# Forty-nine TensorE steps, 115 VectorE steps and 61 ScalarE steps of a hand-ordered decoder layer change places

## The chip, the cores and the metric

The kernel runs on one core of a Trainium2 chip. The metric is the device time of one execution in microseconds (us). Three runs of the kernel before gave 623.32, 624.0 and 621.71 us, a median of 623.32. One more execution was profiled; every row below comes from it.

The engines are named as the profile names them: PE is TensorE (PEld its weight loads), DVE is VectorE, ACT is ScalarE, POOL is GpSimd, SP is SyncE, on whose queue nearly all transfers are issued. "L1591" is line 1591 of the kernel before.

## The reference: what is computed

One layer of a decoder on a sequence of 512 tokens with 1024 features, float32 throughout:

```python
h = rms_norm(x, attn_pre_norm[l])
mix = hybrid_mixer(h, ...)      # differential attention + native sparse attention
x = x + rms_norm(mix, attn_post_norm[l])
h = rms_norm(x, ffn_pre_norm[l])
f = (jax.nn.silu(h @ w_gate[l]) * (h @ w_up[l])) @ w_down[l]
x = x + rms_norm(f, ffn_post_norm[l])
```

`w_gate` and `w_up` are 1024 x 2816, `w_down` is 2816 x 1024. The mixer projects the tokens once, runs four differential-attention heads and eight heads of native sparse attention, and projects back.

## The kernel before, in words

Every float32 operand of a product is split into a high part, rounded to fp32r, and a low part, the remainder, and three fp32r matmuls (high*high, high*low, low*high) stand for one float32 product. So a weight tile goes through a fixed path: a transfer into one of three `raw` slots (512 KB, `load_...`), a copy on ACT that makes the high part (`high_...`), a subtraction on DVE that makes the low part (`low_...`), then the matmuls. A `raw` slot is free for the next transfer when its last reader, often the `low_...` step, is done.

The layer has two parts. The first is the mixer: projections (`F...`, `K...`, `v...`), differential heads (`D...`) and sparse heads (`N...`). The second is the two norms and the feed-forward network (FFN). In the FFN a Strassen-like scheme saves products: of the gate and the up weights of one of 22 column strips f it forms sums (`sum_ff.f.n`, DVE, L1548 to L1555), splits four operands (`high_ff`/`low_ff.f.a, e, b, d`), and runs seven groups of twelve matmuls, `block.f.1` to `block.f.7` (L1591), in two PSUM tiles `yz` and `x`. Between them ACT and DVE combine partial results: `snap_1` and `snap_2` copy PSUM away (ACT, L1601, L1621), `sum_x.f` and `sums.f` add (DVE, L1610, L1626), `gate_x`, `gate_c` apply silu (ACT) and `mult.f` multiplies (DVE, L1632). `block.f.4` adds into what `sums.f` has just read, so it must wait for `sums.f`.

The down projection is a second scheme of the same kind on pairs p of strips. `load_d.f` (L421) and `load_22.p` (L1676) bring pieces of `w_down`; `sums_a.p.0`, `.1`, `.2` (DVE, L1682, L1684, L1688) form sums of them; `left_a`, `right_a` and `high_d`, `low_d` split operands (ACT L1701, L1710, L1714; DVE L1699, L1708, L1720); `product_a.p.n` (six matmuls of 512 columns, L1665) and later `product_b.p.n` and `down.f.i.c` (L1814) accumulate into eight PSUM tiles. `pair_sums.p.n` makes sums of the activations on DVE; its last one also issues two transfers to DRAM, the activation itself (L1654) and a sum (L1658), which `load_b.p` and `load_s4.q` (L1756) read back. At the end `last_sum`, `last_square`, `last_mean`, `last_root`, `last_gain` and `last_row` normalise each of four row blocks and write it out.

The order of all this is written out by hand. `PLAN` lists the 1387 steps of the first part, `PLAN_NORM` and `PLAN_END` the 1198 of the second, and each step is a function that issues its instructions:

```python
ctx.enter_context(tc.manual_schedule())
for tok in plan:
    ops[tok]()
```

Each engine runs its own instructions in the order in which the steps list them, so only the order of steps that share an engine or a queue matters. `PSUM` tiles and the slots `raw`, `hi`, `lo` rotate (3 buffers, `WB`); the tables `HOMES` and `S_HOMES` give each other tile its address.

Of the kernel before, what the change touches and what calls it, by code (L numbers as in the profile page):

```python
# [51 lines left out]
bL4.0 bh4.0 xA2 F0.1.3 F0.2.3 F5.2.4 F2.0.0 F2.1.0 F2.2.0 bl4.0 F5.1.4 xL7 xH7 F5.1.0 F0.0.0 F0.1.0 xL5 xH5 xS4 xl7
xS7 xl5 xS5 F3.0.3 cL F4.1.4 F3.1.3 F3.2.3 F3.0.0 F3.1.0 F3.2.0 F5.0.4 xL6 xH6 bL5.0 cc lL bh5.0 xl6 xA4 F1.1.0 Lv00
F4.2.4 F2.0.4 F2.1.4 F4.2.0 F4.2.5 F3.0.4 F3.1.4 xA5 F1.2.0 F3.2.4 F1.0.4 F1.1.4 xS6 xA6 F5.2.5 xA7 xA1 F0.2.0 bl5.0
rs F3.0.5 rL0 F2.2.4 F2.0.5 F2.1.5 F4.1.0 F2.2.5 rn F5.0.5 F1.2.4 lM rb rL2 F1.0.5 rM2 F1.1.5 F4.0.4 F3.1.5 F3.2.5
F0.0.4 F0.1.4 F0.2.4 F0.0.5 F0.1.5 F0.2.5 F1.2.5 bL7.0 bh7.0 bL6.0 bh6.0 F4.0.5 F5.0.7 rL3 F5.0.6 F4.1.5 F5.2.6
bl7.0 fL12 bl6.0 F5.1.5 rM3 v0h0 v0l0 F5.1.7 F5.2.7 F5.1.6 fR5 F4.0.6 F4.2.7 F4.0.7 F4.1.6 F4.1.7 F4.2.6 fR4 CA
F3.0.6 F3.1.6 F3.2.6 F0.0.6 F0.1.6 F0.2.6 F1.0.6 F1.1.6 F1.2.6 F1.0.7 F1.1.7 K20 Kt0 F2.0.6 F2.1.6 F2.2.6 F2.0.7
Lv01 rL1 rM1 F3.0.7 F1.2.7 LW0 F2.1.7 F0.0.7 F0.1.7 F0.2.7 CW F2.2.7 F3.1.7 F3.2.7 v0h1 v0l1 v0p1.0 W0b v0p3.0
v0p3.1 v0a3 W0d fL10 fh10 KP0 rM0 fR3 W0a W0c fR0 v0p0.0 fR2 pA1 KL1 KP1 KX10 v0p1.1 KW10 v0p2.0 v0p2.1 v0a1 KL0  # L60
Kh10 fl10 v0p0.1 Kl10 Kp10 pH1 fh12 pL1 fR1 pA0 F10.0 pH0 F10.1 F10.2 v0d3 KW11 pL0 fL11 fh11 fl11 fl12 pW1 v0a2
# [2085 lines left out]
```

## Time and profile before

| what | value |
|---|---|
| median of three runs | 623.32 us (621.71 to 624.0) |
| time of the profiled execution | 622.45 us |
| its span, first to last instruction | 620.5 us |
| busy: PE, DVE, ACT, POOL | 607.1, 546.4, 373.9, 101.4 us |
| mean granted TensorE clock | 0.994 of full speed |
| moved by DMA | 98.4 MB, mean 159 GB/s |

The span leaves 1.95 us outside it. A busy PE includes matmuls that run at a lower clock or overlap, so 98% doesn't say that nothing can be gained; the waits and the clock of single stretches say where. A row of the chain of waits gives the start, the duration and the work to which the trace ascribes that stretch. A row of the timeline gives start, duration, engine, line, operation, output<-inputs, shapes and count, and in brackets how long the engine was idle before it and what ended that.

### The profile page before, as it was taken

The numbers are of one execution on the slowest core, as the hardware profiler recorded it, in microseconds if no ns is written. First come the engines' busy times: TensorE is split into PE (matmuls) and PEld (weight loads), VectorE is DVE, ScalarE is ACT, GpSimd is POOL, SyncE is SP. The second block draws the span as 40 slices with busy tenths as digits, with TensorE's granted clock in tenths as the row PEclk, the third lists the DMA queues.
The fourth block names the chain that finished last, engine by engine and source line by source line (L and its number), as shares of the span: only waits on it lengthen the run. The fifth ranks groups of instructions, "written<-read, shape, count | busy, mean of one in ns | idle before, by whom it ended". The sixth has DMA issues, their size and how long they took to land. (4 is left out here: it accounts for less than half of the span.)

```text
span 620.5 us, 10992 instructions
## 1 busy us (share of the span) xinstructions
PE 607.1 (98%) x4065; PEld 549.9 (89%) x4065; DVE 546.4 (88%) x965; ACT 373.9 (60%) x784; POOL 101.4 (16%) x153
## 2 busy tenths in 40 slices
PE   9999999999999999999999999999999799999995
PEld 5888888899999988889999999999999788878884
DVE  5898898997898884999999998899999699899977
ACT  6445375467999986577584565446464365577522
POOL 0030000307868878100000000000000000000000
PEclk9999999999999999999999999999999989999998
DMA  8566986646233211545143434353531554677413
GB/s 263 187 224 248 299 296 230 216 146 248 101 119 101 88 34 63 182 165 203 59 146 104 156 117 136 119 178 121 175 102 54 174 165 140 201 222 252 135 41 130
DMA packets 38341, 98.41 MB, mean 159 GB/s; under 512 B 4240, under 2 KB 11792, under 8 KB 37392
## 3 DMA queue, kind: packets, MB, share of 16 engines
q1 hardware_dynamic: 38144, 97.59, 47.3%
q8 instruction: 32, 0.52, 0.3%
q14 instruction: 21, 0.17, 0.1%
q10 hardware_dynamic: 144, 0.13, 0.1%
HBM read 82.10 MB, written 15.60 MB: 157 GB/s over the span
## 5 line engine op out<-in xcount | busy, mean ns | idle before, releaser
L1867 POOL TENSOR_TENSOR uf<-c,gain 128x512 f32<-128x512 f32 x1 | 1.3, 1277 | 360.1 <-DVE c L1836 360.1
L1055 ACT ACTIVATE p<-sc,nm 128x512 f32<-128x512 f32 (+3 forms) x96 | 50.2, 530 | 14.4 <-DVE nm L1051 12.9
L1051 DVE TENSOR_REDUCE nm<-sc 128x1 f32<-128x384 f32 (+3 forms) x96 | 43.4, 483 | 8.6 <-PE sc L1047 5.5
L1591 PE MATMUL yz<-rope,wbh 128*128 128x256 f32 x352 | 48.0, 280 | 0.0
L1224 POOL TENSOR_TENSOR p<-p,l 128x256 f32<-128x256 f32 (+3 forms) x64 | 45.3, 732 | 1.0
L1591 PEld LDWEIGHTS yz<-rope,wbh 128*128 128x128 f32 x352 | 44.1, 191 | 0.1
L1085 DVE TENSOR_TENSOR ptl<-tr,pth 128x384 fp32r<-128x384 f32 (+1 forms) x60 | 34.3, 592 | 8.4 <-ACT pth L1082 8.4
L1082 ACT ACTIVATE pth<-tr 128x384 fp32r<-128x384 f32 (+1 forms) x60 | 29.9, 530 | 7.3 <-PE tr L1072 6.8
L1568 ACT ACTIVATE whi<-wraw 128x1024 fp32r<-128x1024 f32 x22 | 23.2, 1057 | 13.3 <-DMA wraw<-in_wg 12.5
L1568 ACT ACTIVATE wbh<-wraw 128x1024 fp32r<-128x1024 f32 x22 | 23.3, 1057 | 12.6 <-DVE wraw L1555 7.7
L1576 DVE TENSOR_TENSOR wel<-e,weh 128x1024 fp32r<-128x1024 f32 x22 | 26.7, 1219 | 3.9 <-ACT weh L1568 2.6
L1568 ACT ACTIVATE weh<-e 128x1024 fp32r<-128x1024 f32 x22 | 23.2, 1056 | 8.0 <-DVE e L1550 6.9
L1072 PE MATMUL tr<-ident,p 128*128 128x128 f32 x200 | 27.8, 274 | 0.0
L1714 ACT ACTIVATE whi<-wraw 128x1024 fp32r<-128x1024 f32 x20 | 21.0, 1057 | 10.9 <-PE acc L1665 5.7
L1591 PE MATMUL yz<-rope,wbl 128*128 128x256 f32 x176 | 27.2, 276 | 0.0
L1576 DVE TENSOR_TENSOR wlo<-wraw,whi 128x1024 fp32r<-128x1024 f32 x22 | 26.8, 1217 | 0.0
L1576 DVE TENSOR_TENSOR wbl<-wraw,wbh 128x1024 fp32r<-128x1024 f32 x22 | 26.7, 1217 | 0.0
L1720 DVE TENSOR_TENSOR wlo<-wraw,whi 128x1024 fp32r<-128x1024 f32 x20 | 24.1, 1218 | 1.1 <-ACT whi L1714 1.1
L1621 ACT ACTIVATE us<-yz 128x512 f32<-128x512 f32 x22 | 13.0, 592 | 18.7 <-PE yz L1591 15.7
L1591 PEld LDWEIGHTS yz<-rope,wbl 128*128 128x128 f32 x176 | 23.4, 188 | 0.0
L1041 PE MATMUL sc<-kst,qst 128*128 128x384 f32 (+3 forms) x64 | 23.0, 367 | 0.3 <-DMA kst<-qk 0.3
L1072 PEld LDWEIGHTS tr<-ident,p 128*128 128x128 f32 x200 | 22.4, 141 | 0.7
(382 smaller groups left out, 1993.9 us busy)
## 6 DMA issues: line engine op xcount, KB each, us to landing
wraw<-in_wg SPq DMA_DIRECT2D x24, 512.0 KB, 3.7
wraw<-in_wu SPq DMA_DIRECT2D x22, 512.0 KB, 3.4
wraw<-in_wd SPq DMA_DIRECT2D x22, 512.0 KB, 3.7
qk<-rope SPq DMA_DIRECT2D x7, 1024.0 KB, 5.9
kst<-qk SPq DMA_DIRECT2D x24, 256.0 KB, 4.2
wraw<-in_wf SPq DMA_DIRECT2D x10, 512.0 KB, 4.2
wraw<-in_wo SPq DMA_DIRECT2D x8, 512.0 KB, 4.4
qst<-qk SPq DMA_DIRECT2D x16, 256.0 KB, 2.7
```

What stands on the lines that cost most here:

```text
L1041: pe.matmul(sv[i], lhs, kk[:, 0, :w], start=(n == 0), stop=False, skip_group_check=True)
L1051: dve.tensor_reduce(nm[i], sv[i], AX.X, OP.max, negate=True)
L1055: act.activation(pp[i], sv[i], AF.Exp, bias=nm[i], accum_out=hs["l"][:, row, i:i + 1])
L1072: pe.transpose(tr[:, n * P:(n + 1) * P], pp[i][:, j * P:(j + 1) * P], ident)
L1082: act.activation(part(u, 0), tv[u], AF.Copy)
L1085: dve.tensor_tensor(part(u, 1), tv[u], f32(part(u, 0)), OP.subtract)
L1224: pool.tensor_tensor(p, p, hs["l"][:, 1 + br, i:i + 1].to_broadcast(list(p.shape)), OP.mult)
L1568: act.activation(t[0], w[src], AF.Copy)
L1576: dve.tensor_tensor(t[1], W[f][PARTS[n][0]], f32(t[0]), OP.subtract)
L1591: pe.matmul(o, W[f][w][wi][:, k * P:(k + 1) * P], hop[h][hi][:, k * HS:(k + 1) * HS], start=(n < 3 and m == 0), stop=(m == 11), skip_group ...
L1714: act.activation(hi, oa[f]["raw"], AF.Copy)
L1720: dve.tensor_tensor(lo, o["raw"], f32(o["w"][0]), OP.subtract)
```

## The change

Both plans are written anew with the same steps, and each step also names the spots, in its pools, of the tiles that it makes (`load_d.2:0` puts its tile into spot 0 of `raw`). The rotating buffers and the tables of homes go; a class hands out the named spots. The addresses and the products are the same as before. Counted per engine by the longest common order, 49 of 800 PE steps, 115 of 858 DVE steps, 61 of 624 ACT steps, 9 of 132 POOL steps and 8 of 215 SP steps stand at another place, mostly by a few steps.

```diff
+class Spots:
...
+    def tile(self, shape, dt, tag=None, name=None, bufs=1):
+        if tag in self.tags:
+            return self.pool.tile(shape, dt, tag=f"{tag}.{next(self.turn[0])}", name=name, bufs=1)
+        return self.pool.tile(shape, dt, name=name, bufs=bufs, **({"tag": tag} if tag else {}))
...
+    def run(plan):
+        for step in plan:
+            name, _, spots = step.partition(":")
+            turn[0] = iter(spots)
+            ops[name]()
+            assert not list(turn[0]), step
```

The stretch between the FFN and the down projection, the old order and the new:

```diff
-pair_sums.6.3 load_s4.1 left_a.0.0.0 load_22.1 left_a.0.0.1 right_a.0.0.0 left_a.2.0.0 pair_sums.7.2 snap_2.21
-block.20.6 high_ff.21.b low_ff.21.b block.19.2 high_ff.19.d low_ff.19.d load_d.2 sums_a.1.0 pair_sums.6.4
-pair_sums.7.4 gate_c.17 gate_x.17 mult.17 block.20.5 snap_2.20 high_ff.20.d block.21.2 sums_a.1.1 sum_x.20 load_d.4
-right_a.1.1.0 right_a.1.1.1 sums_a.1.2 high_d.2 low_ff.21.d low_d.2 high_ff.18.d sums.18 low_ff.18.d block.19.4
-block.21.7 load_22.2 load_d.6 sums_a.2.0 right_a.2.1.0 gate_c.19 block.21.3 sums.21 sums_a.2.1 block.20.3 sums_a.2.2
-left_a.6.0.0 right_a.2.1.1 block.18.4 gate_c.18 block.20.7 product_a.0.5 block.21.4 low_ff.20.d sums.20 block.20.4
-left_a.0.1.0 high_d.4 low_d.4 load_22.3 gate_c.21 cut_b.3.2.0 left_a.5.0.0 left_a.0.1.1 product_a.0.7 left_a.2.1.1
-pair_sums.8.1 pair_sums.8.3 sum_x.21 sums_a.3.0 left_a.1.1.0 left_a.1.1.1 product_a.0.1 product_a.1.1 load_b.1
...
+block.17.4 load_22.1:1 pair_sums.6.3 right_a.0.0.0 block.20.6 block.19.2:5 left_a.0.0.1 snap_2.21:n left_a.2.0.0
+pair_sums.7.2 high_ff.21.b:gi high_ff.19.d:ut load_d.2:0 block.20.5 block.21.2:3 low_ff.21.b gate_c.17 load_s4.1:w
+low_ff.19.d gate_x.17 block.19.4 sums_a.1.0 right_a.1.1.0:db pair_sums.6.4:x pair_sums.7.4 snap_2.20:4 mult.17
+block.21.7 load_d.4:2 sums_a.1.1 right_a.1.1.1 sums_a.1.2 block.21.3 block.20.3 sum_x.20:x high_ff.20.d:st
+high_ff.18.d:yv low_ff.21.d load_22.2:1 sums.18:0 high_d.2:2 low_ff.18.d sums_a.2.0 low_d.2:1 sums.21:2 right_a.2.1.0:1i
+block.18.4 left_a.6.0.0:85 sums_a.2.1 block.20.7 sums_a.2.2:g right_a.2.1.1 low_ff.20.d product_a.0.5:27 sums.20:v
+gate_c.19:5 gate_c.18 left_a.0.1.0 block.21.4 left_a.0.1.1 left_a.2.1.1 high_d.4:0 gate_c.21:r load_d.6:0 load_22.3:1
+low_d.4:2 block.20.4 pair_sums.8.1:p sum_x.21 cut_b.3.2.0:n product_a.0.1:43 pair_sums.8.3 load_b.1:u sums_a.3.0
+left_a.5.0.0:61 pair_sums.8.2 product_a.0.7:60 sums_a.3.1 left_a.1.1.0:34 left_a.1.1.1 sums_a.3.2 high_d.6:1 low_d.6:0
```

Five other places that the prediction speaks of: the head, strip 16 of the FFN, `product_a.7.6`, and the end.

```diff
-wu xL1 gc bL1.0 xH1 xl1 bL1.1 bh1.0 F0.0.1 bl1.0 F0.1.1 F0.2.1 bh1.1 bl1.1 F2.0.1 bL1.2 bh1.2 F2.1.1 bl1.2 F2.2.1
...
+xL1:0 bL1.0:0 bh1.0:0 wu:00 gc bL1.1 bl1.0:0 bL1.2 xH1:k F0.0.1:7 bh1.1 F0.1.1 bh1.2 bL2.0:2 F2.0.1:6 xl1:e bl1.1 xS1
...
-low_ff.15.b sums.12 low_ff.16.a low_ff.13.d gate_c.10 block.16.1 snap_1.16 block.16.2 low_ff.16.e block.16.5
...
+block.10.4 sum_ff.16.2 sum_ff.16.4:j low_ff.16.a block.15.6 high_ff.15.b:ac low_ff.11.d low_ff.15.b block.16.1:1
...
+high_d.16:1 low_d.16:0 load_d.1:0 product_a.7.5 left_a.8.0.0 cut_b.1.0.0:c right_a.8.0.0 product_a.7.7 product_a.7.6
...
-last_square.1.0.1 last_gain.1.0 last_mean.1.1 last_root.1 last_row.1.1 last_row.1.0.0 last_row.1.0.1
...
+last_mean.1.0 last_sum.1.0.1 last_mean.1.1 last_square.1.0.1 last_gain.1.0 last_root.1 last_row.1.0.0 last_row.1.1
```

In the old order `low_ff.11.d` stood just ahead of `low_ff.15.b`, and `product_a.8.7`, `.8.1` and `.8.5` ahead of `product_a.7.6`; in the new one `product_a.7.6` is ahead of all three. In the first part the attention products `N5S01` and `D3S10` and the product `Kp10` come some steps later among the matmuls.

## Rows read from the trace of the kernel before

**Rows 1.** The page, busy time by engine.

```profile
PE 607.1 (98%) x4065; PEld 549.9 (89%) x4065; DVE 546.4 (88%) x965; ACT 373.9 (60%) x784; POOL 101.4 (16%) x153
```

**Rows 2.** Stretches of 20 us: length, then busy time and (instructions) of PE, PEld, DVE, ACT, POOL, granted TensorE clock, DMA share, GB/s.

```profile
460.00:480.00 20.00, 20.00 (x175) 19.93 (x174) 19.28 (x30) 10.33 (x17) 0.00 (x0) 1.00 0.23 76
480.00:500.00 20.00, 16.58 (x132) 16.42 (x131) 15.21 (x26) 9.82 (x18) 0.00 (x0) 0.91 0.47 159
```

**Rows 3.** The waits of PE that a semaphore explains, over the whole span: us in total, times, longest.

```profile
PE yz L1591 <- DVE vs L1626: 3.4, 1, 3.4
...
PE yz L1591 <- DVE wlo L1576: 0.5, 1, 0.5
PE sc L1041 <- DMA kst<-qk: 0.3, 1, 0.3
PE fm L691 <- DVE wlo L684: 0.3, 1, 0.3
```

**Rows 4.** The chain of waits that ended last: start, us, what.

```profile
462.87 2.14 DMA wraw<-in_wu
...
482.58 5.57 DMA wraw<-in_wd
...
489.64 2.11 DMA s<-s
...
495.96 4.59 PE yz L1591 x24
...
607.69 0.69 DVE c L1836
```

**Rows 5.** The timeline of DVE from 478 to 500 us.

```profile
479.96 1.22 DVE L1720 TENSOR_TENSOR wlo<-wraw,whi 128x1024 fp32r<-128x1024 f32 x1
...
488.25 0.69 DVE L1682 TENSOR_TENSOR wraw<-wraw 128x512 f32<-128x512 f32 x1 [3.73 <-DMA wraw<-in_wd]
...
491.85 0.43 DVE L1610 TENSOR_TENSOR act<-x,snap 128x256 f32<-128x256 f32 x1 [1.03 <-DMA s<-s]
...
493.99 1.22 DVE L1720 TENSOR_TENSOR wlo<-wraw,whi 128x1024 fp32r<-128x1024 f32 x1
495.13 0.68 DVE L1626 TENSOR_TENSOR vs<-yz,us 128x512 f32<-128x512 f32 x1
495.73 0.68 DVE L1576 TENSOR_TENSOR dl<-d,dh 128x512 fp32r<-128x512 f32 x1
```

**Rows 6.** The timeline of SP's queue from 478 to 500 us: when each transfer is issued.

```profile
481.69 0.33 SPq L1756 DMA_DIRECT2D s4b<-s  x1
482.11 0.38 SPq L1676 DMA_DIRECT2D wraw<-in_wd  x1
482.58 0.38 SPq L421 DMA_DIRECT2D wraw<-in_wd  x1
483.01 0.90 SPq L1654 DMA_DIRECT2D x<-act  x2
```

**Rows 7.** The timeline of PE from 478 to 500 us.

```profile
487.39 0.62 PE L1591 MATMUL yz<-x22l,dh 128*128 128x256 f32 x4
487.84 0.62 PE L1591 MATMUL yz<-x22h,dl 128*128 128x256 f32 x4
...
491.92 0.62 PE L1591 MATMUL yz<-rope,wbl 128*128 128x256 f32 x4
495.96 0.74 PE L1591 MATMUL yz<-x22h,dh 128*128 128x256 f32 x4 [3.42 <-DVE vs L1626]
```

**Rows 8.** The timeline of PE from 498 to 512 us.

```profile
500.38 0.40 PE L1665 MATMUL acc<-whi,sh 128*128 128x512 f32 x1
...
503.20 0.63 PE L1591 MATMUL yz<-x22h,dh 128*128 128x256 f32 x4
...
504.61 0.40 PE L1665 MATMUL acc<-th,sh 128*128 128x512 f32 x1
...
506.01 0.39 PE L1665 MATMUL acc<-whi,sh 128*128 128x512 f32 x1
```

**Rows 9.** The timeline of DVE from 498 to 512 us: `sums.20`, `sum_x.21` and what follows it.

```profile
500.58 0.69 DVE L1626 TENSOR_TENSOR vs<-yz,us 128x512 f32<-128x512 f32 x1 [0.38 <-PE yz L1591]
...
504.32 0.42 DVE L1610 TENSOR_TENSOR act<-x,snap 128x256 f32<-128x256 f32 x1
504.65 0.68 DVE L1682 TENSOR_TENSOR wraw<-wraw 128x512 f32<-128x512 f32 x1
```

**Rows 10.** The page, DMA issues: count, KB each, median us from issue to landing.

```profile
wraw<-in_wd SPq DMA_DIRECT2D x22, 512.0 KB, 3.7
```

**Rows 11.** The timeline of PE from 543 to 549 us.

```profile
546.36 0.40 PE L1665 MATMUL acc<-th,sl 128*128 128x512 f32 x1
546.89 0.50 PE L1665 MATMUL acc<-tl,sh 128*128 128x512 f32 x1
```

**Rows 12.** The timelines of PE and DVE around strip 16.

```profile
424.64 0.74 PE L1591 MATMUL yz<-x11h,wlo 128*128 128x256 f32 x4 [0.51 <-DVE wlo L1576]
...
423.38 1.22 DVE L1576 TENSOR_TENSOR wlo<-wraw,whi 128x1024 fp32r<-128x1024 f32 x1
```

**Rows 13.** The timeline of PE at the head.

```profile
10.01 0.97 PE L691 MATMUL fm<-xh,whi 128*128 128x512 f32 x3
```

**Rows 14.** The timeline of DVE from 607 to 620 us: the gain (`last_gain.1.0`) of the last row block.

```profile
614.09 0.69 DVE L1867 TENSOR_TENSOR uf<-c,gain 128x512 f32<-128x512 f32 x1
```

More of the change, by code (lines that the diff above doesn't have):

```diff
@@ L52 @@
[L52 to L61, printed above, removed]
@@ L177 @@
-block.19.3 high_ff.21.e low_ff.21.e gate_c.14 sum_x.15 gate_x.15 mult.14 sum_x.17 block.21.1 high_ff.21.d
-sum_ff.21.3 gate_c.15 mult.15 block.21.5 snap_1.21 load_22.0 snap_1.20 load_d.0 sums_a.0.0 right_a.0.1.0 sums_a.0.1
-sums_a.0.2 block.19.7 sums.19 block.20.2 block.21.6 sums.17 block.17.4 right_a.0.1.1 high_d.0 low_d.0 pair_sums.7.1
-pair_sums.6.3 load_s4.1 left_a.0.0.0 load_22.1 left_a.0.0.1 right_a.0.0.0 left_a.2.0.0 pair_sums.7.2 snap_2.21
-block.20.6 high_ff.21.b low_ff.21.b block.19.2 high_ff.19.d low_ff.19.d load_d.2 sums_a.1.0 pair_sums.6.4
@@ L187 @@
-pair_sums.8.1 pair_sums.8.3 sum_x.21 sums_a.3.0 left_a.1.1.0 left_a.1.1.1 product_a.0.1 product_a.1.1 load_b.1
-left_a.4.1.0 load_b.3 product_a.1.7 product_a.2.7 sums_a.3.1 high_d.6 gate_c.20 pair_sums.8.2 load_s4.3 left_a.2.0.1
-load_s4.2 left_a.1.0.0 product_a.2.1 load_d.8 sums_a.3.2 right_a.3.0.0 low_d.6 right_a.1.0.0 cut_b.7.2.0
-right_a.0.0.1 right_a.3.1.0 right_a.3.0.1 pair_sums.7.3 right_a.3.1.1 left_a.3.1.0 left_a.1.0.1 sum_x.19
-right_a.1.0.1 load_22.4 sums_a.4.0 product_a.0.6 product_a.1.6 left_a.3.0.0 left_a.3.0.1 sums_a.4.1 sums_a.4.2
@@ L192 @@
-pair_sums.5.3 right_a.4.1.0 right_a.4.1.1 product_a.1.5 gate_x.20 product_a.2.5 product_a.3.5 load_d.10
-right_a.2.0.0 left_a.3.1.1 product_a.3.7 load_b.4 left_a.4.0.0 left_a.4.0.1 high_d.8 product_a.3.1 low_d.8
-cut_b.1.1.0 right_a.4.0.0 right_a.2.0.1 load_22.5 sums_a.5.0 right_a.5.1.0 sums_a.5.1 product_a.2.6 product_a.3.6
-high_d.10 right_a.4.0.1 product_a.4.6 sums_a.5.2 right_a.5.0.0 left_a.8.1.0 right_a.5.1.1 load_b.5 left_a.7.1.0
-left_a.4.1.1 product_a.4.5 left_a.5.0.1 load_d.12 load_22.6 low_d.10 product_a.5.5 left_a.5.1.0 product_a.4.1
@@ L197 @@
-left_a.5.1.1 product_a.5.1 sums_a.6.0 sums_a.6.1 sums_a.6.2 product_a.4.7 product_a.5.7 right_a.6.1.0 load_d.14
-right_a.6.1.1 left_a.6.0.1 cut_b.5.1.0 high_d.12 low_d.12 load_s4.0 cut_b.0.2.0 cut_b.0.2.1 load_22.7 right_a.5.0.1
-sums_a.7.0 left_a.7.0.0 cut_b.4.2.0 sums_a.7.1 load_b.2 right_a.6.0.0 right_a.6.0.1 load_d.16 sums_a.7.2
-product_a.5.6 right_a.7.1.0 right_a.7.1.1 product_a.6.5 left_a.6.1.0 left_a.6.1.1 cut_b.2.2.0 high_d.14 low_d.14
-left_a.7.1.1 gate_x.18 product_a.6.1 mult.18 gate_x.19 load_b.7 left_a.7.0.1 cut_act.18.0 left_a.8.1.1 product_a.6.7
@@ L202 @@
-right_a.7.0.0 product_a.6.6 product_a.7.1 load_d.3 product_a.7.5 sums_b.1 high_d.3 load_22.8 sums_a.8.0
-right_a.8.1.0 cut_b.2.1.0 low_d.3 sums_a.8.1 sums_a.8.2 high_d.16 right_a.7.0.1 load_b.0 right_a.8.1.1 product_a.7.7
-product_a.8.7 load_kept.3 low_d.16 product_a.8.1 load_d.1 cut_act.18.1 left_a.8.0.0 left_a.8.0.1 product_a.8.5
-cut_b.1.0.0 load_d.5 load_kept.0 product_a.7.6 right_a.8.0.0 right_a.8.0.1 cut_b.1.2.0 load_d.9 sums_b.0 cut_b.6.2.0
-cut_b.6.2.1 high_d.1 low_d.1 mult.20 sums_b.2 part_of_sum.5.0 load_d.15 part_of_sum.1.0 product_a.8.6 cut_b.2.2.1
@@ new lines @@
+sum_x.18:8 low_ff.17.d low_ff.14.d pair_sums.2.3 sum_ff.20.1:c gate_c.16 high_ff.20.a:10 left_a.2.1.0:f0 sum_ff.20.2
+sum_ff.20.4:7 snap_2.18:5 block.17.7 low_ff.20.a sum_ff.20.3 high_ff.19.e:ig load_ff.21.g:1 high_ff.20.b:jc block.18.3
+pair_sums.6.1:m low_ff.19.e block.18.7 low_ff.15.d load_ff.21.u:2 block.20.1:1 pair_sums.3.3 sums.14:q high_ff.20.e:bd
+block.19.1:6 low_ff.20.e pair_sums.6.2 high_ff.21.a:02 sum_ff.21.1:e sum_ff.21.2 mult.16 sum_ff.21.4:0 block.19.5
+snap_1.19:a block.15.4 block.19.6 snap_2.19:t high_ff.21.e:gi low_ff.21.a low_ff.20.b block.14.4 low_ff.21.e gate_c.14
@@ new lines @@
+block.19.3 block.21.1:4 load_22.0:1 sum_x.15:v gate_x.15 load_d.0:0 high_ff.21.d:rz mult.14 gate_c.15 block.19.7
+sum_x.17:6 sum_ff.21.3 mult.15 block.21.5 sums_a.0.0 sums_a.0.1 right_a.0.1.0:ea block.20.2:7 snap_1.21:l sums.19:q
+sums_a.0.2:2 sums.17:z snap_1.20:y high_d.0:1 left_a.0.0.0:h9 right_a.0.1.1 low_d.0:0 pair_sums.7.1:d block.21.6
+block.17.4 load_22.1:1 pair_sums.6.3 right_a.0.0.0 block.20.6 block.19.2:5 left_a.0.0.1 snap_2.21:n left_a.2.0.0
+pair_sums.7.2 high_ff.21.b:gi high_ff.19.d:ut load_d.2:0 block.20.5 block.21.2:3 low_ff.21.b gate_c.17 load_s4.1:w
@@ new lines @@
+low_d.4:2 block.20.4 pair_sums.8.1:p sum_x.21 cut_b.3.2.0:n product_a.0.1:43 pair_sums.8.3 load_b.1:u sums_a.3.0
+left_a.5.0.0:61 pair_sums.8.2 product_a.0.7:60 sums_a.3.1 left_a.1.1.0:34 left_a.1.1.1 sums_a.3.2 high_d.6:1 low_d.6:0
+product_a.1.1 product_a.1.7 left_a.4.1.0:74 gate_c.20 left_a.1.0.0 load_b.3:4 left_a.2.0.1 pair_sums.7.3
+right_a.3.0.0:cj product_a.2.7 right_a.1.0.0 right_a.0.0.1 load_s4.3:z cut_b.7.2.0:h right_a.3.0.1 load_d.8:2
+left_a.1.0.1 load_s4.2:7 right_a.3.1.0 right_a.3.1.1 sum_x.19 product_a.2.1 left_a.3.1.0:59 product_a.0.6:15
@@ new lines @@
+product_a.1.5 left_a.3.0.0 load_22.4:0 sums_a.4.0 right_a.1.0.1 right_a.4.1.0:ea gate_x.20 load_d.10:1 product_a.1.6
+sums_a.4.1 right_a.2.0.0 left_a.3.0.1 sums_a.4.2:h load_b.4:b right_a.4.1.1 pair_sums.5.3 left_a.4.0.0 left_a.3.1.1
+left_a.4.0.1 product_a.2.5 high_d.8:2 low_d.8:1 load_22.5:0 right_a.2.0.1 sums_a.5.0 sums_a.5.1 sums_a.5.2 product_a.3.5
+cut_b.1.1.0:3 right_a.5.1.0:bd right_a.4.0.0 product_a.3.7 product_a.2.6 load_b.5:y right_a.5.1.1 high_d.10:0
+load_d.12:2 left_a.4.1.1 load_22.6:0 left_a.5.0.1 product_a.3.1 right_a.4.0.1 low_d.10:2 right_a.5.0.0 sums_a.6.0
@@ new lines @@
+product_a.3.6 load_d.14:1 left_a.8.1.0:06 product_a.4.6 left_a.7.1.0:i1 sums_a.6.1 left_a.5.1.0 right_a.6.1.0:fc
+right_a.6.1.1 sums_a.6.2:j load_s4.0:f left_a.5.1.1 left_a.6.0.1 cut_b.5.1.0:9 high_d.12:1 cut_b.0.2.0:m low_d.12:0
+product_a.4.5 right_a.5.0.1 left_a.7.0.0 product_a.5.5 load_22.7:0 cut_b.4.2.0:l right_a.6.0.0 cut_b.0.2.1 product_a.4.1
+sums_a.7.0 product_a.4.7 right_a.7.1.0:ea right_a.6.0.1 load_b.2:e product_a.5.1 sums_a.7.1 left_a.6.1.0 right_a.7.1.1
+cut_b.2.2.0:9 sums_a.7.2 high_d.14:2 load_d.16:2 product_a.5.7 product_a.5.6 left_a.6.1.1 low_d.14:1 left_a.7.1.1
@@ new lines @@
+load_b.7:s load_d.3:0 product_a.6.5 gate_x.18 product_a.6.1 mult.18 left_a.7.0.1 gate_x.19 left_a.8.1.1 sums_b.1
+cut_act.18.0:g product_a.6.7 right_a.7.0.0 product_a.6.6 load_22.8:1 high_d.3:0 sums_a.8.0 low_d.3:2 sums_a.8.1
+sums_a.8.2:5 right_a.7.0.1 product_a.7.1 right_a.8.1.0:db load_b.0:t load_kept.3:f cut_b.2.1.0:4 right_a.8.1.1
+high_d.16:1 low_d.16:0 load_d.1:0 product_a.7.5 left_a.8.0.0 cut_b.1.0.0:c right_a.8.0.0 product_a.7.7 product_a.7.6
+product_a.8.7 product_a.8.1 cut_act.18.1:o load_d.5:1 cut_b.1.2.0:1 left_a.8.0.1 high_d.1:2 load_kept.0:8 product_a.8.5
@@ new lines @@
+right_a.8.0.1 cut_b.6.2.0:0 sums_b.0 product_a.8.6 low_d.1:1 part_of_sum.5.0:i part_of_sum.1.0:k cut_b.6.2.1 load_d.9:2
+sums_b.2 mult.20 cut_b.2.2.1 part_of_sum.5.1:d cut_b.1.2.1 high_d.5:1 product_b.0.5 cut_b.3.2.1 product_b.1.5
+cut_b.2.0.0:a part_of_sum.7.1:f cut_b.3.1.0:7 cut_b.2.1.1 cut_b.5.2.0:j low_d.5:0 load_d.15:0 cut_b.1.1.1 cut_b.0.1.0:6
+cut_b.0.1.1 sums_b.7 product_b.2.5 cut_act.20.0:8 part_of_sum.1.1:w cut_b.3.1.1 product_b.0.1 load_d.7:1 gate_x.21
+cut_b.0.0.0:d cut_b.0.0.1 pair_sums.8.4:3 product_b.1.1 sums_b.3 cut_b.1.0.1 product_b.2.1 high_d.9:2 part_of_sum.7.0:e
@@ L233 @@
+last_row.1.0.1
 """
@@ L413, in hybrid_block_kernel @@
     cpool.tile([P, 16], F32, name="cpad")
-    wpool = ctx.enter_context(tc.tile_pool(name="weights", bufs=3))
+    turn = [None]
+    wpool = Spots(ctx.enter_context(tc.tile_pool(name="weights", bufs=1)), ("raw", "hi", "lo"), turn)
+    for tag in ("raw", "hi", "lo"):
+        wpool.first(tag, "012", [P, 1024])
     zpool = ctx.enter_context(tc.tile_pool(name="edge", bufs=1, side="right"))
```

517 lines of the change are left out of this document (190 added, 327 removed).

## The prediction

> **What bounds the kernel now.** I read the busy line of the page, then the stretches of 20 us, then the waits of PE, then the chain of waits back from the end, then the timelines of the places that these name. PE is busy 607.1 of 620.5 us [rows 1]. The FFN stretch shows PE at 20.00 of 20 and DVE at 19.28 [rows 2]: there PE is the bound and DVE has almost no room behind it. One stretch stands out: from 480 to 500 PE is busy 16.58 us, DVE only 15.21, at a granted clock of 0.91 [rows 2]. The list of PE's waits says the same: 3.4 us in one piece on `sums` (L1626), and nothing else in it that these steps touch above 0.5 [rows 3].
>
> The chain shows why: a `w_down` load that took 5.57 us, a spill that took 2.11, and then matmuls [rows 4]. In the timelines: DVE stands idle 3.73 us for that load and starts `sums_a.1.0` at 488.25, stands idle 1.03 us for the spill before `sum_x.20` at 491.85, runs `low_d.2` at 493.99, and only then, at 495.13, `sums.18` [rows 5]. PE is through with everything ahead of `block.18.4` at 491.92 + 0.45 = 492.37 (four matmuls of this kind take 487.84 - 487.39 = 0.45) and starts it at 495.96 [rows 7]. So 3.59 us are lost. Then the clock: the next 24 matmuls take from 495.96 to 500.38, 4.42 us [rows 7, 8], where at 0.1125 each they take 2.70: 1.72 us more. After its idle time PE ran at the lower level (1.2 GHz) for a while. Together the place costs 5.31 us.
>
> After the last matmul a chain on DVE runs from 607.69 to the end [rows 4], some 10 us that only its own order can shorten.
>
> **The change part by part.** All instructions stay, so only waits can go or come.
>
> *The load, on SP.* Before, `load_s4.1` goes out at 481.69, as soon as the slot it writes is free, and behind it, in SP's order, `load_22.1` at 482.11 and `load_d.2` at 482.58 [rows 6]. `load_22.1` and `load_d.2` need `raw` slots, which `right_a.0.1.1` and `low_d.0` free; `low_d.0` starts at 479.96 and takes 1.22, so it ends at 481.18 [rows 5]. In the new order both loads stand ahead of `load_s4.1`, so `load_d.2` can go out at about 481.2, 1.38 us earlier. Upper end: it also lands 1.38 earlier, at 486.8. Lower end: it lands when it did (0), since the same bytes share the DMA engines. Both ends stay in the range; I take 1.35, because the loads after the move have less ahead of them than before. What is queued behind on SP: `load_s4.1`, whose data are wanted only by `cut_b` steps of the down projection's second half, and the two spills of `pair_sums.6.4` and `7.4`, which are ready far later than SP.
>
> *What the trace makes of a rule here.* The same kind of load took 2.14 us where nothing was issued near it, 3.7 in the median, and 5.57 here with 0.5 MB issued just ahead and two spills issued just behind [rows 4, 6, 10]. The Trainium skill ("DMA: Bandwidth & Descriptors", section "Queues, rings and completion order") says that each DMA engine consumes one queue's descriptors in ring order, so that what stands behind a load should not delay it. By that rule alone the three transfers, 1 MB from 481.69 on, would at the rate of the lone load have been done by about 486.0; they were done at 488.15, so here the trace doesn't agree, and what is issued behind counts too. By the rule, moving `load_s4.1` behind would bring another 1 us at this place, and the sum below would be about 1 us larger; by the rows it brings none. I go by the rows.
>
> *DVE between the load and `sums.18`.* A step of 512 columns advances DVE by 495.73 - 495.13 = 0.60 [rows 5], one of 256 by 504.65 - 504.32 = 0.33 [rows 9], a `low` of 1024 by 495.13 - 493.99 = 1.14 [rows 5]. Starting at 486.9: `sums_a.1.0`, two `pair_sums`, `mult.17`, `sums_a.1.1`, and then, in the new order, `right_a.1.1.1` and `sums_a.1.2` ahead of `sum_x.20`: 5 x 0.60 + 2 x 0.33 brings DVE to 490.6 where `sum_x.20` could start. Its spill, issued 0.03 after `pair_sums.7.4` (at about 488.2) and 2.11 long, lands at 490.3: the idle 1.03 us are covered by the two steps put ahead. Then `sum_x.20`, `low_ff.21.d`, and `sums.18` ahead of `low_d.2`: 0.33 + 0.60 + 0.68 ends at 492.2. PE wants it at 492.37. So the stall of 3.59 goes, and the lower clock's 1.72 with it. With a load that lands only 0.47 earlier (one issue on SP), `sums.18` ends at 493.1 and 0.7 to 0.9 us of stall stay; whether the clock then falls no row shows, the stalls of 0.3 to 0.5 elsewhere left it at 1.00.
>
> *What is late next.* `low_d.2` now lies behind `sums.18`, and PE comes to what follows sooner. `block.20.4` needs `sums.20`: from 492.2 DVE has eight steps of 0.60 and `low_d.2` (1.14) up to `sums.20`'s end: 498.2 to 498.6. PE is there at 503.20 - 5.31 = 497.89 [rows 8] and waits about 0.85 with the semaphore's time. Then the second half of `product_a.0.1`, which is put ahead of `product_a.0.7`, needs the PSUM tile that `sum_x.21` reads. DVE reaches it by two `left_a`, `low_d.4`, one `pair_sums`: 498.6 + 2 x 0.60 + 1.14 + 0.33 + 0.42 = 501.7. PE would be there at 500.2 + 0.7 = 500.9 and waits 0.9. One step later `left_a.1.1.1` costs another 0.2. So 5.31 - 0.85 - 0.9 - 0.2 = 3.35 us stay from this place: DVE's own chain now sets PE's time. Bounds: 5.31 (DVE was further ahead already) and 1.9 (the load lands as late as before: all of DVE 1.4 later).
>
> *`product_a.7.6`.* At 546.89 PE waits for DVE: the matmul before it starts at 546.36 and these take 0.23, so 0.30 is lost, and a little more in the next [rows 11]. In the new order `product_a.7.6` (1.40 long, [rows 8]) goes ahead and covers it: 0.42. Bounds 0 and 0.42.
>
> *Places before 480.* Strip 16: PE waits 0.51, 0.78 by start to start, for `low_ff.16.a`, which runs on DVE at 423.38 [rows 12] and stands three steps (0.60 + 1.14 + 0.60 = 2.34) earlier after: this wait goes, and `low_ff.15.b` and what follows come 1.14 later. The 0.3 on a `kst` load and the 0.3 at the head [rows 3] go as well, but at the head PE stops again at 10.01 for the next load [rows 13], which is no earlier. What PE wins here it brings to 492 only if DVE comes there earlier too, and DVE is 19.28 of 20 busy [rows 2] and bound by the same chain of loads. Bounds +1.6 and -1.0 (some steps of strips 3, 15, 17, 18 go later by 0.6 to 2.5); I take 0.
>
> *The end.* `last_mean.1.1` goes ahead of `last_gain.1.0` (0.60, [rows 14]), so the root may start earlier: between 0 and 0.60, I take 0.25.
>
> **The sum.** 3.35 + 0.42 + 0.25 = 4.0 us off the profiled execution, which took 622.45 with 1.95 outside its span: 618.4. The median of the runs is 0.87 higher: 619.3 from there. I say 619.0.
>
> **The rivals.**
>
> *All waits go* (615). DVE reaches 484 earlier, by what strip 16 and others free, and the two new stalls don't come. Then 5.31 + 0.42 + 0.25 + about 2 from the earlier places: 8.0 off 623.3. For it: every wait of PE in the list is one that a moved step addresses. Against it: DVE at 15.21 of 20 in that stretch is idle only for the load and the spill [rows 2, 5], and once these are gone it is full. Chance 0.14.
>
> *The wait only moves* (621.3). The load lands at 488 as before because the DMA engines carry the same bytes, and the reordered steps of the mixer and of strips 3 to 4 add waits of some tenths (`rM1` ahead of `CA`, `tr31` and `tr30` ahead of `block.3.1`). Then 1.9 + 0.4 - 0.3 = 2.0 off. For it: 5.57 us for one load shows that the DMA engines were crowded. Chance 0.24.
>
> *The loads of the FFN come late* (626.5), the case on the other side. One mechanism: a promoted step pushes a `low_ff` that frees a `raw` slot, the next strip's load is issued that much later, and with DVE at 19.28 of 20 nothing is caught up. The pushes are about 2.5, 1.2, 1.14 and 0.6 us (strips 3, 18, 15, 17). If all count and nothing is won, 5.4 are added; if half, 2.7: 626 to 628.7. It decides where a load lands later than DVE's turn for it; a load takes 3.7 in the median [rows 10], and PE's list has no wait in the FFN that a load caused [rows 3], which speaks against it. Chance 0.12.
>
> That the named spots add waits of their own, because a slot is tracked otherwise than a rotating buffer, would show as small stalls everywhere; I count it in the second rival.
>
> **How the numbers follow.** The forecast (617.5 to 620.3, its own range from the bounds of the load and the end) has 0.50. A measurement here tells 0.5%, 3.1 us, from no change: faster is below 620.2, slower above 626.4. Faster: nearly all of the forecast (0.47), the first rival (0.14), a little of the second (0.04): 0.65. Slower: half or more of the last, 0.08. The rest, 0.27, is the same. The range from 615.0 to 623.6 leaves out the last rival and the far ends.
>
> **What would show it.** In the timeline after: `load_d.2` issued near 481.2 and `sums_a.1.0` near 486.9; no idle DVE before `sum_x.20`; `block.18.4` with a gap under 0.5; the clock of 480 to 500 at 1.00; new short waits of PE ahead of `block.20.4` on L1626 and in `product_a.0.1` on L1610; no gap at `product_a.8.7`. Wrong if DVE still waits for `wraw<-in_wd` until 488, if 480 to 500 keeps a clock below 1, or if PE's waits in the FFN (L1591 on L1576) grow beyond the 0.5 of before.

## The result and the profile after

The changed kernel took 616.11 us in the median of four runs (615.93 to 619.16), the kernel before 623.28 beside them: a ratio of 0.990, 95% interval 0.9864 to 0.9936. The forecast was 619.0 with 615.0 to 623.6. It is faster, by 7.2 us in the medians and by 622.45 - 616.08 = 6.4 in the two profiled executions, where 4.0 had been worked out.

The page of the kernel after, busy times and the granted clock in 40 slices, then the waits of PE (us in total, times, longest). They answer to [rows 1, 3]:

```profile
PE 604.1 (98%) x4065; PEld 547.6 (89%) x4065; DVE 545.9 (89%) x965; ACT 373.4 (61%) x784; POOL 101.5 (17%) x153
...
PEclk9999999999999999999999999999999999999999
```

```profile
PE warm L424 <- DVE warm L421: 1.2, 1, 1.2
PE fm L572 <- ACT whi L562: 0.8, 1, 0.8
PE acc L1548 <- DVE act L1493: 0.6, 1, 0.6
PE cmp L804 <- DVE wlo L795: 0.3, 1, 0.3
```

The line numbers are lower by 112 to 119, since the tables of homes are gone. The 3.4 us on `sums` are no longer there, nor the 0.5 on `low_ff.16.a`. New are 0.8 at the head, 0.3 in the mixer (L804) and 0.6 of a product (L1548) on `sum_x` (L1493): the wait that the prediction placed in `product_a.0.1`. The stretches of 20 us, which answer to [rows 2]:

```profile
460.00:480.00 20.00, 20.00 (x179) 20.00 (x178) 19.27 (x31) 11.16 (x20) 0.00 (x0) 1.00 0.24 75
480.00:500.00 20.00, 19.37 (x157) 18.33 (x156) 17.90 (x30) 10.37 (x19) 0.00 (x0) 1.00 0.62 204
```

PE is busy 19.37 us there instead of 16.58, at full clock, and DVE has 2.7 us more work in it.

Now where along the kernel the time came from. The table takes the start of a PE step in the two timelines, at places ahead of which PE has done the same set of steps in both.

| PE step | before | after | after minus before |
|---|---|---|---|
| `F6.1` (mixer) | 89.23 | 90.27 | +1.04 |
| `D3Q10` (mixer) | 206.36 | 206.57 | +0.2 |
| `B1.1` (FFN begins) | 294.15 | 294.87 | +0.7 |
| `block.16.2` | 425.22 | 424.09 | -1.1 |
| `block.17.4` | 480.08 | 478.49 | -1.6 |
| `block.18.4` | 495.96 | 490.73 | -5.2 |
| `product_a.1.1` | 507.40 | 501.61 | -5.8 |
| `product_a.8.6` | 552.06 | 546.07 | -6.0 |
| end of the span | 620.5 | 614.3 | -6.2 |

So 1.6 us were there before the handover, 4.0 more came up to `product_a.7.1` (-5.6 at 541), 0.4 at `product_a.7.6`, 0.2 at the end. The timelines of SP and of DVE of the kernel after show the handover; they answer to [rows 5, 6]:

```profile
478.19 0.33 SPq L1559 DMA_DIRECT2D wraw<-in_wd  x1
479.33 0.33 SPq L309 DMA_DIRECT2D wraw<-in_wd  x1
480.05 0.33 SPq L1639 DMA_DIRECT2D s4b<-s  x1
```

```profile
483.16 0.69 DVE L1565 TENSOR_TENSOR wraw<-wraw 128x512 f32<-128x512 f32 x1 [0.37 <-DMA wraw<-in_wd]
...
488.55 0.42 DVE L1493 TENSOR_TENSOR act<-x,snap 128x256 f32<-128x256 f32 x1 [1.61 <-DMA s<-s]
...
489.60 0.69 DVE L1509 TENSOR_TENSOR vs<-yz,us 128x512 f32<-128x512 f32 x1
```

The load of `load_d.2` is issued at 479.33 instead of 482.58 and used 3.83 us later instead of 5.67; DVE waits 0.37 instead of 3.73 for it. `sums.18` starts at 489.60, in time. The spill wait before `sum_x.20` did not go, it grew from 1.03 to 1.61. And PE, which answers to [rows 7, 8]:

```profile
490.73 0.62 PE L1474 MATMUL yz<-x22h,dh 128*128 128x256 f32 x4
...
496.41 0.74 PE L1474 MATMUL yz<-x22h,dh 128*128 128x256 f32 x4
...
499.42 0.51 PE L1548 MATMUL acc<-whi,sh 128*128 128x512 f32 x1 [0.63 <-DVE act L1493]
```

`block.18.4` starts without a gap. `block.20.4` (496.41) is 0.16 late, and the second half of `product_a.0.1` waits 0.63; with a short wait right behind it in `product_a.1.1` that place costs 0.98 start to start (from the start of one matmul to that of the next, less what that takes at full pace). These are the waits that the prediction had put there.

### The profile page after: what moved, and what is told of

It is laid out like the page before. It is cut to its first block, busy times and chain, and to the rows that moved or that the text cites. A ratio compares the mean times of both kernels' runs of the same rounds, so it can differ in the third digit from the quotient of the medians.

```text
span 614.3 us, 11002 instructions
## 1 busy us (share of the span) xinstructions
PE 604.1 (98%) x4065; PEld 547.6 (89%) x4065; DVE 545.9 (89%) x965; ACT 373.4 (61%) x784; POOL 101.5 (17%) x153
## 4 chain that ended last, share of the span: by engine, by line
PE 86%; DVE 8%; DMA 3%; ACT 1%; issue 1%; SPq 0%; DVEq 0%
PE yz L1474 25%; PE acc L1548 13%; PE fm L589 9%; PE mix L1221 5%; PE x L1474 4%; PE fm L572 4%; PE tr L953 4%; PE avn L1136 3%; PE g L705 2%; PE sc L922 2%; PE sc L923 2%; PE mixp L1207 2%; PE v L705 2%; PE cmp L804 1%; PE av L1014 1%; PE acc L1697 1%
## 5 line engine op out<-in xcount | busy, mean ns | idle before, releaser
L936 ACT ACTIVATE p<-sc,nm 128x256 f32<-128x256 f32 (+3 forms) x96 | 50.2, 530 | 13.8 <-DVE nm L932 13.5
```

What stands on the lines that cost most here:

```text
L936: act.activation(pp[i], sv[i], AF.Exp, bias=nm[i], accum_out=hs["l"][:, row, i:i + 1])
```

## The experiments

Twelve kernels ran, each timed in five rounds beside the kernel before. "old" and "new" are the two orders of a plan; the second plan was cut at places where old and new have issued the same set of steps: after `block.15.1` (529 steps), `block.16.1` (552), `gate_c.14` (705) and `sum_x.19` (839). All use the new form with named spots. With the old order this form issues the same instructions with the same waits on every engine as the kernel before, so the named spots can cost nothing. Microseconds off the kernel before are worked out from the ratio.

**The handover alone.**

```diff
-PLAN_NORM = old
+PLAN_NORM = old[:705] + new[705:839] + old[839:]
```

> The old order everywhere but in one stretch of the second plan, from after gate_c.14 to sum_x.19 (some 473 to 512 us), which has the new order. Theory A (each stretch is worth what its own waits cost): 4.0 us off the kernel before, ratio 0.9935, PE starts block.18.4 near 492.4 with a gap under 0.3 and the clock stays at 1.00 there. Rival B (the lead won in the FFN was needed for the loads to go early enough): less than 2.5 us off, ratio above 0.996, and a gap of 1 us or more at block.18.4.

618.8 us, ratio 0.9942 (0.992 to 0.9963). Theory A holds for the size, 3.6 us, and the gap that rival B wanted at `block.18.4` isn't there. PE in this run:

```profile
493.14 0.62 PE L1478 MATMUL yz<-x22h,dh 128*128 128x256 f32 x4
...
499.58 0.74 PE L1478 MATMUL yz<-x22h,dh 128*128 128x256 f32 x4 [0.76 <-DVE vs L1513]
...
502.59 0.50 PE L1552 MATMUL acc<-whi,sh 128*128 128x512 f32 x1 [0.62 <-DVE act L1497]
```

`block.18.4` has no gap, but `block.20.4` waits 0.76 for `sums.20` and `product_a.0.1` 0.62 for `sum_x.21`. Start to start, and with the short wait behind the second, they cost 0.91 and 0.98. The prediction had 0.85 and 0.9 + 0.2.

**The handover undone.**

```diff
-PLAN_NORM = new
+PLAN_NORM = new[:705] + old[705:839] + new[839:]
```

> The new order everywhere but in the same stretch, which has the old one. Theory A: 4.0 us slower than the kernel after, ratio to before 0.9950, with the stall at sums.18 of 3.4 us and the clock below 1 again. Rival B (the FFN's lead is lost in the stall, because the loads there go out when they did): ratio 0.999 to 1.000.

620.11 us, ratio 0.9958 (0.9935 to 0.9982): the rest of the change brings 2.6 us by itself, and the 3.3 us wait on `sums` is back, with a clock of 0.91 from 480 to 500. Rival B falls.

**Only the FFN.**

```diff
-PLAN_NORM = old
+PLAN_NORM = new[:705] + old[705:]
```

> The new order in the second plan up to gate_c.14 (norms and FFN, some 250 to 473 us), the old order before and behind. Theory A: PE leads by 1.7 us at 473, DVE and the loads of the handover lead by as much because they wait for PE's blocks, and the end comes 1.7 us sooner: ratio 0.9973. What my prediction assumed (a lead won in the FFN is not brought past 492): ratio 1.000, PE's lead of 1.7 us gone at block.18.4.

621.86 us, ratio 0.9981 (0.9964 to 0.9998). In its trace PE leads by 1.7 us at 474 (`block.19.7`, 1.69 earlier than before), and the handover moves with it: `load_s4.1` goes out at 479.79 instead of 481.69 and `load_d.2` at 480.69 instead of 482.58. PE in the handover:

```profile
494.02 0.71 PE L1478 MATMUL yz<-x22h,dh 128*128 128x256 f32 x4 [3.38 <-DVE vs L1513]
494.57 0.63 PE L1478 MATMUL yz<-x22l,dh 128*128 128x256 f32 x4
...
496.93 0.39 PE L1552 MATMUL acc<-whi,sh 128*128 128x512 f32 x1
```

The stall is as long as before (3.38, before 3.42) but starts earlier, so the lead passes through it: my assumption that it is lost at 492 was wrong. The time alone hardly decides this (1.2 us off, between 0.1 and 2.2); the trace does. The next 24 matmuls took 496.93 - 494.02 = 2.91 us here, where before they took 4.42: in this execution the clock hardly fell. The last section comes back to that.

**Only strip 16.**

```diff
-PLAN_NORM = old
+PLAN_NORM = old[:529] + new[529:552] + old[552:]
```

> The new order only from after block.15.1 to block.16.1 (low_ff.16.a three steps earlier on DVE). Theory A: the wait of 0.5 us (0.78 start to start) ahead of block.16.1's third group goes, and the lead of 0.78 reaches the end: ratio 0.9988. What my prediction assumed: the wait goes and the lead is gone at block.18.4, ratio 1.000.

622.38 us, ratio 0.9988 (0.997 to 1.0007). The time can't tell this from no change; the trace can. From `block.5.5` to `block.16.2` PE goes from 0.71 behind the kernel before to 0.07 ahead, which is the 0.78 of [rows 12], and at `block.18.4` it is 0.82 ahead: the lead is kept through the stall here too.

**Only the first part.**

```diff
-PLAN = old
+PLAN = new
```

> The new order of the first plan alone (mixer, up to some 245 us). Theory A, from the lead of PE in the two traces: 0.2 to 0.4 us slower than before, ratio 1.0005; up to 1.0 us behind near 90 us and most of it made good by 206 us. Rival: the mixer's order is worth something of its own that the rest hides, ratio below 0.998.

622.4 us, ratio 0.9988 (0.997 to 1.0006). And from the other side, the kernel after with the old first plan:

```diff
-PLAN = new
+PLAN = old
```

> The old order in the first plan, the new one in the second. Theory A: the first plan's order is worth 0 within what a run can show, ratio 0.989 to 0.991. Rival: it costs the 0.4 us that PE of the kernel after is behind at 206 us and 1.0 at 90 us: ratio 0.9885 or less.

616.51 us, ratio 0.9901 (0.9874 to 0.9927). The mixer's new order is worth nothing that can be measured either way.

**Only the down projection and the end.**

```diff
-PLAN_NORM = old
+PLAN_NORM = old[:839] + new[839:]
```

> The new order from after sum_x.19 to the end (some 512 us on) alone. Theory A: the gap of 0.3 us ahead of the third matmul of product_a.8.7 goes (0.4 with the next) and the end after PE's last matmul is 0.2 shorter: 0.6 us off, ratio 0.9990. Rival: the gap comes back at another product, ratio 1.000.

621.82 us, ratio 0.9973 (0.9959 to 0.9987). In the trace PE wins 0.44 us against the kernel before between `product_a.0.5` and `product_a.8.6`, as expected; the runs say 1.7, with 0.8 at the near end of the interval. Another 0.43 lies between `product_a.8.6` and the end of the span (68.03 us instead of 68.47), so the trace accounts for 0.87. What the rest would be is open.

**One step of the handover: the order of three loads.**

```diff
-... pair_sums.6.3 load_s4.1 left_a.0.0.0 load_22.1 ... low_ff.19.d load_d.2 sums_a.1.0 ...
+... pair_sums.6.3 left_a.0.0.0 load_22.1 ... low_ff.19.d load_d.2 load_s4.1 sums_a.1.0 ...
```

> The kernel before with one step moved: load_s4.1 behind load_d.2 on SP, nothing else. Theory A: load_d.2 goes out at 481.2 and, with only load_22.1 ahead of it, lands in 3.8 to 4.4 us instead of 5.57, so sums_a.1.0 starts near 485.4 and sums.18 ends near 493.5 (the spill's wait and low_d.2 still stand ahead of it): stall 1.0 to 1.4 us, clock loss perhaps gone: 2.2 to 4 us off, ratio 0.9935 to 0.9965. Rival C (the bytes share the DMA engines, the order of issue hardly moves the landing): sums_a.1.0 at 486.9 or later, stall above 2 us, ratio above 0.9975.

618.93 us, ratio 0.9932 (0.9915 to 0.995): 4.2 us off by one moved step, no less than the whole handover. SP, DVE and PE of this run:

```profile
480.19 0.33 SPq L1564 DMA_DIRECT2D wraw<-in_wd  x1
481.33 0.33 SPq L314 DMA_DIRECT2D wraw<-in_wd  x1
481.71 0.42 SPq L1644 DMA_DIRECT2D s4b<-s  x1
```

```profile
485.75 0.69 DVE L1570 TENSOR_TENSOR wraw<-wraw 128x512 f32<-128x512 f32 x1 [1.11 <-DMA wraw<-in_wd]
489.69 0.42 DVE L1498 TENSOR_TENSOR act<-x,snap 128x256 f32<-128x256 f32 x1 [1.36 <-DMA s<-s]
```

```profile
493.80 0.69 PE L1479 MATMUL yz<-x22h,dh 128*128 128x256 f32 x4 [1.41 <-DVE vs L1514]
...
496.60 0.40 PE L1553 MATMUL acc<-whi,sh 128*128 128x512 f32 x1
```

`load_22.1` goes out at 480.19 instead of 482.11, since it no longer stands behind a read-back that waits for its slot until 481.69. So the issue of `load_d.2` comes 1.25 us earlier, the load is used 4.42 us after it instead of 5.67, and DVE starts 2.50 earlier. A wait of 1.41 us stays at `block.18.4`, with the clock up (24 matmuls in 2.80), and after it PE waits nowhere in the handover: `block.20.4` and `product_a.0.1` come without a gap. So PE loses 1.56 us once, where the new order of DVE and ACT loses 0.91 and 0.98 a little later.

**The new handover with the old order of the loads.**

```diff
-... left_a.0.0.0:h9 right_a.0.1.1 low_d.0:0 pair_sums.7.1:d block.21.6 block.17.4 load_22.1:1 ... load_s4.1:w ...
+... left_a.0.0.0:h9 right_a.0.1.1 low_d.0:0 pair_sums.7.1:d block.21.6 block.17.4 load_s4.1:w load_22.1:1 ...
```

> The new order in the handover alone, as in the first run, but load_s4.1 again ahead of load_22.1. Theory A: the load lands near 488.2 as before, sums.18 is 1.14 + 1.03 us earlier for DVE's order, a stall of some 1.3 us stays at block.18.4: 1.5 to 3.5 us off, ratio 0.9945 to 0.9975. Rival C: as good as the first run within 0.5 us.

621.22 us, ratio 0.9958 (0.9941 to 0.9975). The load is used 5.46 us after its issue again. PE waits three times, for 1.23, 1.0 and 1.0 us start to start, 3.3 in all, hardly less than the one stall of before (3.59): without the loads, the order of DVE and ACT only spreads the wait. Short waits did not bring the clock down (1.00 in this stretch), which is worth the 1.7 us that the clock cost before; that is most of what this kernel gains.

**That one step put back in the kernel after, and that one step alone kept.**

```diff
-... block.17.4 load_22.1:1 ... load_d.2:0 ... load_s4.1:w ...
+... block.17.4 load_s4.1:w load_22.1:1 ... load_d.2:0 ...
```

> The kernel after with one step put back: load_s4.1 ahead of load_22.1 on SP. The load then lands some 5.5 us after its issue instead of 3.8 and is issued 1.2 later, so sums_a.1.0 starts 2.9 us later than in the kernel after; PE loses 2 to 3.3 us in all between block.18.4 and product_a.0.1, of which 1.1 were lost already: 1.5 to 2.5 us slower than the kernel after, ratio 0.9925 to 0.9945. If the order on DVE and ACT is what counts: ratio 0.990 to 0.991.

618.8 us, ratio 0.9939 (0.9917 to 0.9962), 2.4 us slower than the kernel after by the ratios and 2.7 by the medians, at the same lead of PE up to `block.17.4` within 0.6. DVE waits again:

```profile
486.25 0.69 DVE L1570 TENSOR_TENSOR wraw<-wraw 128x512 f32<-128x512 f32 x1 [4.01 <-DMA wraw<-in_wd]
```

```diff
-PLAN_NORM = new
+PLAN_NORM = new[:705] + old_with_load_s4.1_behind_load_d.2[705:839] + new[839:]
```

> The kernel after with the old order between gate_c.14 and sum_x.19 on all engines, but load_s4.1 behind load_d.2. If that one step on SP is the whole of the handover's gain, as the run with it alone suggests: within 0.6 us of the kernel after, ratio 0.989 to 0.991, with one stall of some 1.5 us at block.18.4 and none at block.20.4 and product_a.0.1. If the other steps add their own 1 to 2 us: ratio 0.992 to 0.9935.

615.88 us, ratio 0.9895 (0.9865 to 0.9925): as fast as the kernel after.

```profile
491.35 0.71 PE L1479 MATMUL yz<-x22h,dh 128*128 128x256 f32 x4 [1.31 <-DVE vs L1514]
```

Of all the moved steps in the handover, one on SP's queue carries the gain; those of DVE and ACT turn one wait of 1.5 us at `block.18.4` into two later ones with a sum of 1.1 to 1.9.

**All traces beside each other.** The fourteen traces can be compared by stretches, from the start of one PE step to the start of another, ahead of which the old and the new order have done the same steps. Times are in us, the number of traces in parentheses. The version of the next paragraph is left out of the handover, and the run with strip 16 alone counts as new in the row of strip 16 and is left out of the one above it.

| stretch | old order | new order |
|---|---|---|
| `B1.1` to `block.17.4` (FFN) | 185.3 to 186.5 (6) | 183.6 to 184.2 (7) |
| of it `block.5.5` to `block.16.2` (strip 16) | 88.9 to 89.3 (6) | 88.4 (8) |
| `block.17.4` to `product_a.7.1` (handover) | 60.2 to 62.9 (6) | 57.9 to 58.6 (3) |
| the same, only the load order new | | 58.1, 58.2 |
| the same, all new but the load order | | 60.1, 60.6 |
| `product_a.7.1` to `product_a.8.6` | 9.7 (4), 10.0, 10.1, 10.6 | 9.7 (7) |
| `product_a.8.6` to the end | 68.5 (6), 68.8 | 68.0 to 68.2 (7) |

The FFN's order is worth 1.0 to 2.9 us, in the means 1.9. In the handover the load order alone gives as much as all of the new order. The order of DVE and ACT alone (60.1, 60.6) is no better than the old order in the one execution whose clock hardly fell (60.2). And the gap that `product_a.7.6` was to cover is missing in four of the seven traces with the old order there too, so the 0.4 of the two kernels' traces is not shown to be the change's.

**A version past both.** In the kernel after DVE stands idle 1.61 us for the spill, and `low_d.2` (1.14) stands behind it. It can be put into that gap:

```diff
-... sums_a.1.1 right_a.1.1.1 sums_a.1.2 ... sum_x.20:x ... sums.18:0 high_d.2:2 low_ff.18.d sums_a.2.0 low_d.2:1 ...
+... sums_a.1.1 high_d.2:2 right_a.1.1.1 sums_a.1.2 low_d.2:1 ... sum_x.20:x ... sums.18:0 low_ff.18.d sums_a.2.0 ...
```

> The kernel after with two steps moved: high_d.2 behind sums_a.1.1 on ACT and low_d.2 behind sums_a.1.2 on DVE, into the 1.61 us in which DVE of the kernel after waits for the spill ahead of sum_x.20. If DVE's chain after sums.18 is what stops PE in product_a.0.1 (0.63 us) and at block.20.4 (0.15), both waits go and the end comes 0.8 to 1.1 us sooner: 615.2 against 616.1, ratio to before 0.9885. Rival: sum_x.21 waits for block.21.4 or for a load instead and PE's wait stays: no change.

615.72 us, ratio 0.9888 (0.986 to 0.9916), the lowest of all, but the time can't tell it from the kernel after (0.9864 to 0.9936). The trace shows a gain: between `block.18.4` and `product_a.0.7` PE wins 0.84 us against the kernel after.

```profile
487.54 1.23 DVE L1608 TENSOR_TENSOR wlo<-wraw,whi 128x1024 fp32r<-128x1024 f32 x1
488.68 0.42 DVE L1498 TENSOR_TENSOR act<-x,snap 128x256 f32<-128x256 f32 x1
```

```profile
496.25 0.63 PE L1479 MATMUL yz<-x22h,dh 128*128 128x256 f32 x4
...
498.42 0.50 PE L1553 MATMUL acc<-whi,sh 128*128 128x512 f32 x1
```

`low_d.2` now ends where `sum_x.20` starts without a wait; `block.20.4` (496.25) has no gap, and the second half of `product_a.0.1` starts 0.29 after the matmul before it, where 0.23 is the pace. The load took 5.1 us in this execution and left 0.29 us of waiting at `block.18.4`; over the whole handover 0.4 us are won against the kernel after (57.45 and 57.85).

## Why the prediction came out as it did

The time lies inside the range and the sign is right; the forecast was 2.9 us too slow. By its terms:

| term of the sum | predicted | in the traces |
|---|---|---|
| places before 480 | 0 | 1.6 |
| handover, with the clock | 3.35 | 4.0 |
| `product_a.7.6` | 0.42 | 0.4 |
| the end | 0.25 | 0.2 |
| sum | 4.0 | 6.2 |

- *The step that failed: "what PE wins here it brings to 492 only if DVE comes there earlier too ... I take 0".* The condition was right and it is met. `load_s4.1` waits for `block.17.4`, and DVE's steps of the FFN wait for PE's blocks, so a PE that is ahead pulls loads and DVE along. The run with the FFN alone and the run with strip 16 alone both show the lead on the far side of the stall. So a term that was put at 0 is worth 1.6 in the two kernels' traces, the far end of the bounds given for it, and the FFN's share of it 1.0 to 2.9 over all traces. A busy share of 19.28 of 20 says that DVE has little slack, not that it sets the pace.
- *The load.* The issue was placed right (1.38 us earlier by order; 1.25 in the run with that step alone). The landing was not: I let it shift with the issue, and it shortened as well. In all eight traces with `s4b` ahead the load is used 5.4 to 5.9 us after its issue; in the six with `s4b` behind it, 3.8 to 5.1. Counted from `block.17.4`, it was used after 8.17 us before and after 4.67 in the kernel after: 3.5 us sooner, where I had counted 1.35. The spill's wait took part of that back. That the handover gave 4.0 instead of 3.35 isn't shown to come from this: with the same order it took 57.85, 58.07 and 58.57 us in three executions, a spread as large as the difference, and against the mean of the six old ones (61.65) the three give 3.5.
- *The rule that I set aside.* The Trainium skill ("DMA: Bandwidth & Descriptors", section "Queues, rings and completion order") says that each DMA engine consumes descriptors in ring order. The shorter times with `s4b` behind the load agree with that. That what stands behind a load costs it nothing was my own conclusion: the section adds that a later descriptor may finish its write before an earlier one. The trace of before spoke against the conclusion (488.15 instead of 486.0), not against the order, and I set both aside.
- *"Whose data are wanted only by `cut_b` steps of the down projection's second half".* Too far off: in the kernel after the read-back is issued at 480.05 and its first copy runs at 496.73, 17 us later, still far enough. The timeline of ACT:

```profile
496.73 0.41 ACT L1660 ACTIVATE s4r<-s4b 128x256 fp32r<-128x256 f32 x1
```

- *`sum_x.20`'s wait "covered by the two steps put ahead".* Wrong. The spill took 3.97 us in the kernel after (issued at 484.55; `sum_x.20` starts at 488.55) instead of 2.11, and DVE waited 1.61. It cost little because `sums.18` still came in time. The size is that of one execution: with the same order here and the old first part the spill took 2.83 and DVE waited 0.47.
- *"DVE's own chain now sets PE's time", with waits of 0.85, 0.9 and 0.2 at `block.20.4`, `product_a.0.1` and `product_a.1.1`.* Right in place and, in the run with the handover alone, in size (0.91, and 0.98 for the last two). In the kernel after, where the load came sooner, 0.16 and 0.98.
- *What the text gave the credit for.* I spent most of the working on the order of DVE's steps. The runs show no gain of it beside the load order: 615.88 without it, 616.11 with it.
- *`product_a.7.6`.* The 0.42 came out as forecast, but by luck: four of seven traces with the old order have no such gap, so the new order would have had nothing to cover there.
- *The rivals.* "All waits go" came nearest in time (615) but not in mechanism: the waits at `block.20.4` and `product_a.0.1` did come. "The wait only moves" is what the handover with old loads does. The late loads of the FFN did not appear: PE is at 20.00 of 20 in every stretch from 300 to 480.

## What to carry to other kernels

Ask of a long wait on a load first what stands ahead of it in its queue and who needs that: here a 256 KB read-back, wanted 17 us later, held the load that a block of PE waited for, and one moved line was worth 4.2 us by itself. Reordering compute behind a late transfer mostly moves the wait to the next consumer: here one wait of 3.6 us became three with a sum of 3.3, and most of what that kernel gained came from the clock, which stayed up. And a lead won upstream is lost at a stall only if the stall's cause does not move with it: follow what the late transfer itself waits for.
